# Long passes in the last feed-forward, a shift made on TensorE, and a new order of modulation units, in a two-block float32 model

## The chip, the cores and the metric

The kernel runs on one core of a Trainium2 chip. A core has five engines that each take their own instructions in order and meet through semaphores: TensorE (PE in the rows; its weight loads are PEld), VectorE (DVE), ScalarE (ACT), GpSimd (POOL) and SyncE (SP), and 16 DMA engines. The metric is the device time of one execution in microseconds (us); the kernel before takes 2502.35 us, the median of three runs (2498.07 to 2504.37).

## The reference

One sequence of 256 tokens of 1024 features, all in float32, passes two blocks. The first has two layers: a norm with a modulation, then attention (layer 0) or a gated DeltaNet (layer 1), and a feed-forward. The second block carries the 256 tokens and 256 context tokens through two layers of feed-forward, mixing (Fourier, convolution and latent attention) and feed-forward; the last layer leaves the context behind after its mixing.

```python
def first_block(...):
    cond = jax.nn.silu(c)
    for layer in range(DEPTH):
        mod = (cond @ ada_w[layer] + ada_b[layer])[:, None, :]
        shift_m, scale_m, gate_m, shift_f, scale_f, gate_f = jnp.split(mod, 6, axis=-1)
        h = rmsnorm(x, norm_mix_g[layer]) * (1.0 + scale_m) + shift_m
        ...
        x = x + gate_m * mixed
        h = rmsnorm(x, norm_ffn_g[layer]) * (1.0 + scale_f) + shift_f
        x = x + gate_f * swiglu(h, ffn_w_in[layer], ffn_w_out[layer])
    return rmsnorm(x, final_norm_g)

def ffn_half_step(s, m, i, norm_g, w_in, w_out):
    h = modulate(rmsnorm_2(s, norm_g), m, i)
    gu = h @ w_in
    y = (jax.nn.silu(gu[..., :D_FF]) * gu[..., D_FF:]) @ w_out
    return s + 0.5 * gate(m, i) * y
```

The feed-forward is 2816 wide. The modulations are products of one vector with a 1024 x 1024 matrix for each of 6 chunks a layer (first block) and of two vectors (tokens, context) for each of 9 (second block).

## The kernel before

**Tiles.** Activations lie with features on the 128 partitions: x is 8 tiles of 128 features by 256 tokens (512 columns where the context stands beside). A float32 product is made of three: each weight is split into a rounded part (hi, cast by ScalarE, L378) and the rest (lo, subtracted by VectorE, L379), each activation likewise, and `mm3` issues hi·hi (L405), hi·lo (L406) and lo·hi (L407) into one accumulator. So a group of one 128 x 128 weight tile and one activation tile takes three passes, of 256 columns for the tokens alone and 512 with the context.

**The stream of weights.** `plan()` writes one list of units of up to 128 x 1024 numbers (512 KB). SP's queue loads them in that order into a ring of 9 buffers (`pump`, L361, up to 12 units ahead), and the next three "mat" units are split. `get(key)` hands over the unit that a product needs; the list must be in the order of the calls. A "mod" unit is 128 columns of a modulation matrix: `mod_unit` (L480) has VectorE multiply it with the condition, spread over all partitions, and sum each row (L491, then a read of the accumulator); in the second block twice. `_evenly` (L48) puts the mod units between the mat units of a stage, `flush` works off those that stand next in the list before the next product is issued. Since VectorE takes its work in order, the place in the list decides what a mod product delays.

**Stages, by the profile's time.** Start, to 45 us: the condition is broadcast by one DMA to 128 partitions, the positions too; the first 16 units are the scale and the shift of layer 0's first norm; x is squared, POOL and VectorE add the squares; the first product reads h = x·scale·r + shift (`shift`, L855, with L860, L861). Attention to 180. First feed-forward to 380. Gated DeltaNet to 640: projections and heads 0 to 3 to 455, the inverse of their matrices together with heads 4 to 7 to 545, then z, the second inverse and the output. Feed-forward to 820. The second block's feed-forwards and mixings with 512 columns to 2290. The last feed-forward, for the tokens alone, to 2485, and the last norm.

**The last feed-forward** (`ffn`, L623, with `ns` = 1) multiplies the weights with x·gain, before it is divided by the root of the mean square; two more columns carry the shift (258 in all), and `act_raw` (L629) multiplies the result with r, adds the shift's column (copied by ScalarE, one column, L632) and applies the gate. The hidden width comes in thirds of 8, 7 and 7 tiles (j = 0 to 21); for each j a gate unit and an up unit, behind each third 8 output units (`project_out`, L602), whose result `resid` (L599) adds to x. The first two j are made together (`lead`). The last mixing's output projection (8 units of 8 tiles, on 256 columns) uses `project_out` as well. `push` (L532) squares each finished x tile on ScalarE and adds them on POOL; `rsq` (L515) makes r; `scaled` (L1404) multiplies each x tile with gain and r in one VectorE operation (L1409), and 8 DMAs write the result (L1522).

## Time and profile before

| | |
|---|---|
| runs, median (lowest to highest) | 2502.35 us (2498.07 to 2504.37) |
| profiled execution, its own time | 2497.55 us |
| span of the instructions in it | 2495.7 us |
| mean granted TensorE clock | 0.994 of 2.4 GHz |

All views below come from that one profiled execution; what lies around its span is 1.85 us. A row of a timeline is: start, duration, engine, line, operation, result and inputs by the program's names (numbers of buffers left out), and in brackets the time that the engine had waited and what released it. "x3" are instructions put together. A pass of TensorE is shown with its own length, from issue to end; passes overlap, so a stream's cost is the distance between starts. Busy time of an engine is not work that sets the end.

### The profile page before, as it was taken

To read this page: it belongs to the slowest core of one execution; us is meant where nothing else is said; L and a number is where in the kernel's file an instruction comes from. 1 tells how busy PE (TensorE), PEld (TensorE's weight loads), DVE (VectorE), ACT (ScalarE), POOL (GpSimd) and SP (SyncE) were. 2 spreads that over 40 slices of the span, in tenths; PEclk is the share of its full clock that TensorE was granted. 3 is DMA by queue.
4 is the path that set the end of the run, shared out by engine and by line. 5 is a ranking of instruction groups with operands and counts; after the bars stand their busy time and mean duration, and the time that the engine had idled before them with its cause. 6 is when DMAs were issued, how large, how long until landed. Compare 5 with 4: busy or idle time off the path is not lost.

```text
span 2495.7 us, 38415 instructions
## 1 busy us (share of the span) xinstructions
PE 2391.3 (96%) x14963; PEld 2130.3 (85%) x14963; DVE 1786.3 (72%) x3087; ACT 1073.5 (43%) x1879; POOL 169.9 (7%) x172
## 2 busy tenths in 40 slices
...
GB/s 332 271 223 227 225 236 225 153 102 90 263 265 209 161 236 191 173 162 99 79 79 33 85 219 178 153 182 87 109 201 180 160 175 95 83 131 77 205 183 70
DMA packets 118406, 412.21 MB, mean 165 GB/s; under 512 B 13136, under 2 KB 16464, under 8 KB 118224
## 3 DMA queue, kind: packets, MB, share of 16 engines
...
## 4 chain that ended last, share of the span: by engine, by line
PE 76%; DVE 9%; DMA 8%; issue 3%; ACT 2%; POOL 1%; DVEq 0%; ACTq 0%; SPq 0%; POOLq 0%
PE pmm L405 21%; PE pmm L406 21%; PE pmm L407 21%; DMA r<-w 7%; DVE l L379 2%; DVE r L491 2%; DVE junk L491 2%; PE pax L1026 2%; PE pmm L1348 1%; PE pax L407 1%; PE pax L406 1%; PE pax L405 1%; PE pnm L1387 1%; PE pax L1358 1%; ACT h L378 1%
## 5 line engine op out<-in xcount | busy, mean ns | idle before, releaser
L378 ACT CAST h<-r 128x1024 fp32r<-128x1024 f32 (+2 forms) x543 | 549.6, 1017 | 992.4 <-PE pmm L406 907.3
L379 DVE TENSOR_TENSOR l<-r,h 128x1024 fp32r<-128x1024 f32 (+2 forms) x543 | 645.0, 1192 | 195.6 <-ACT h L378 188.2
L405 PE MATMUL pmm<-h,h 128*128 128x512 f32 (+1 forms) x1916 | 668.3, 350 | 31.3 <-ACT h L860 23.1
L406 PE MATMUL pmm<-h,h 128*128 128x512 f32 (+1 forms) x1916 | 664.7, 347 | 1.8 <-DVE h L593 1.6
L407 PE MATMUL pmm<-h,l 128*128 128x512 f32 (+1 forms) x1916 | 662.3, 346 | 0.0
L405 PEld LDWEIGHTS pmm<-h,h 128*128 128x128 f32 x1916 | 364.1, 190 | 78.1 <-ACT h L860 23.8
L406 PEld LDWEIGHTS pmm<-h,h 128*128 128x128 f32 x1916 | 364.2, 190 | 48.5 <-DVE h L593 3.7
L407 PEld LDWEIGHTS pmm<-h,l 128*128 128x128 f32 x1916 | 364.2, 190 | 44.7 <-issue 0.2
L405 PE MATMUL pmm<-hid,h 128*128 128x256 f32 (+1 forms) x1053 | 349.8, 332 | 6.2 <-DVE s L633 2.7
L406 PE MATMUL pmm<-hid,h 128*128 128x256 f32 (+1 forms) x1053 | 348.3, 331 | 1.5 <-DVE hid L444 1.5
L407 PE MATMUL pmm<-hid,l 128*128 128x256 f32 (+1 forms) x1053 | 348.0, 331 | 0.7 <-DVE l L379 0.7
L405 PE MATMUL pmm<-hb,h 128*128 128x258 f32 x1008 | 286.4, 284 | 5.7 <-ACT hb L581 4.2
L407 PE MATMUL pmm<-hb,l 128*128 128x258 f32 x1008 | 284.9, 283 | 0.0
L406 PE MATMUL pmm<-hb,h 128*128 128x258 f32 x1008 | 284.9, 283 | 0.0
L491 DVE SCALAR_TENSOR_TENSOR junk<-r,cnd 128x1024 f32<-128x1024 f32 x144 | 175.9, 1221 | 125.9 <-DMA r<-w 122.6
L405 PEld LDWEIGHTS pmm<-hid,h 128*128 128x128 f32 x1053 | 200.4, 190 | 26.3 <-ACT hid L443 3.9
L406 PEld LDWEIGHTS pmm<-hid,h 128*128 128x128 f32 x1053 | 200.4, 190 | 20.9 <-DVE hid L444 2.4
L407 PEld LDWEIGHTS pmm<-hid,l 128*128 128x128 f32 x1053 | 200.5, 190 | 19.3 <-DVE l L379 1.1
L405 PEld LDWEIGHTS pmm<-hb,h 128*128 128x128 f32 x1008 | 190.8, 189 | 7.3 <-ACT hb L581 5.0
L406 PEld LDWEIGHTS pmm<-hb,h 128*128 128x128 f32 x1008 | 191.7, 190 | 0.4 <-DVE hb L582 0.2
L407 PEld LDWEIGHTS pmm<-hb,l 128*128 128x128 f32 x1008 | 191.7, 190 | 0.1
L491 DVE SCALAR_TENSOR_TENSOR r<-r,cnd 128x1024 f32<-128x1024 f32 x144 | 176.1, 1223 | 5.5 <-ACT cnd L464 2.4
...
## 6 DMA issues: line engine op xcount, KB each, us to landing
r<-w SPq DMA_DIRECT2D x665, 512.0 KB, 4.2
...
cnd<-cond ACTq DMA_DIRECT2D x8, 512.0 KB, 4.6
...
x<-xT ACTq DMA_DIRECT2D x8, 128.0 KB, 5.7
x<-ctxT ACTq DMA_DIRECT2D x8, 128.0 KB, 2.6
```

The lines of the kernel that those rows point to most:

```text
L378: nc.scalar.copy(h[:, :n], r[:, :n])
L379: nc.vector.tensor_tensor(lo[:, :n], r[:, :n], h[:, :n].bitcast(F32), op=OP.subtract)
L405: nc.tensor.matmul(out, wh, ah, start=start, stop=False)
L406: nc.tensor.matmul(out, wh, al, start=False, stop=False)
L407: nc.tensor.matmul(out, wl, ah, start=False, stop=stop)
L491: nc.vector.scalar_tensor_tensor(o, r, 1.0, self.conds[ns - 1 + s], op0=OP.mult, op1=OP.mult, accum_out=t[:, 8 * s + m:8 * s + m + 1])
L1026: nc.tensor.matmul(p[:, s], a[:, s], b[:, s], start=True, stop=True)
L1348: self.nc.tensor.matmul(s, q, k, start=True, stop=True)
L1358: self.nc.tensor.transpose(p[:, 128 * b:128 * b + 128], P[:, 128 * b:128 * b + 128], self.ident)
L1387: nc.tensor.matmul(o[64 * a:64 * a + 64, 128 * qt:128 * qt + 128], V[2 * s + b][:, h], pts[a][:, 128 * b:128 * b + 128], start=b == 0, sto ...
```

## The change

1. *Last feed-forward and last mix projection.* `wide` holds the two parts of an activation side by side as one tile of 512 columns. For each weight tile it issues one pass of hi with all 512 columns (L480: hi·hi in the left half, hi·lo in the right) and one of lo with 256 (L481, into the left half). The halves are added where the result is read: `act_wide` copies one half on ScalarE and adds on VectorE, `resid_wide` adds to x twice. It is used from j = 4 on; `enter_wide` makes the normalised activations for it. The last two output units of the last third and of the mix projection stay with three passes.
2. *Last norm.* x·gain is made on ScalarE for each tile as x is finished; behind r stand one product for each tile, six on VectorE and two (tiles 1 and 4) on POOL, and the output DMAs in another order.
3. *Start.* The condition and the positions are loaded as one row each and spread by a product with a row of ones. Each of the eight scale sums is finished as it comes. The eight shift units are loaded as rows of the matrix and multiplied on TensorE (`mod_rows`), four products of 32 rows by 256 columns each; a copy, two transposes and an addition bring the sum to its columns. The sums of squares are made on TensorE. The x tiles come over two queues. The first constants are loaded behind 19 units instead of first. The first projection's unit stands before the last two of the eight.
4. *Places of the mod units.* `_place` gives each stage's units a room, and spreads the mods by it. The chunk-2 mods of layer 1 (8 units) move from the DeltaNet into the first feed-forward. In the DeltaNet, heads 0 to 3 hold none instead of 10, heads 4 to 7 18 instead of 8, z 6 as before, the output none instead of 8. The second block's feed-forwards hold more of theirs among the output units.

The diff, cut to its core:

```diff
-def _evenly(units, mods, a, b):
-    n = len(units) - a - b
-    out, k = [], 0
-    for i, u in enumerate(units):
+def _place(units, mods, room):
+    room = [room(i, u[1]) for i, u in enumerate(units)]
+    out, k, c, total = [], 0, 0.0, sum(room)
+    for u, w in zip(units, room):
         out.append(u)
-        while k < len(mods) and i >= a + k * n // len(mods):
+        c += w
+        while k < len(mods) and c * len(mods) >= (k + 1 - 1e-6) * total:
             out.append(mods[k])
             k += 1
+    assert k == len(mods)
...
-    u += _evenly(q, A(0, 2, 3, 4), 4, 0)
+    rows = [("rows", ("ada_w", 0, 0, kt), [("ada_w", 0, kt * 128, 0, 1024)]) for kt in range(KT)]
+    u = A(0, 1) + rows[:6] + q[:1] + rows[6:] + _place(q[1:], A(0, 2, 3, 4), lambda i, key: float(i >= 3))
...
-    u += _evenly(q[:16], A(0, 5), 2, 3) + _evenly(q[16:], A(1, 0, 1), 0, MODS_OUT)
+    u += _place(q[:16], A(0, 5), _ffn_room(2, 15)) + _place(q[16:], A(1, 0, 1, 2), _ffn_room(0, 46))
...
-    u += _evenly(q, A(1, 2, 3, 4, 5), 0, 4)
...
+    u += _place(q, A(1, 3, 4, 5), lambda i, key: 2.0 if key[0] in "qkv" and key[1] > 3 else float(key[0] == "z"))
...
+    def wide(self, units, h):
+        ps = [(self.ax if i % 2 else self.mm)() for i in range(len(units))]
+        k = len(h)
+        for j, a in enumerate(h):
+            for u, p in zip(units, ps):
+                s = slice(128 * j, 128 * j + 128)
+                self.nc.tensor.matmul(p, u.hi[:, s], a.both, start=j == 0, stop=False)
+                self.nc.tensor.matmul(p[:, :T], u.lo[:, s], a[0], start=False, stop=j == k - 1)
+        return ps
...
-        if m == KT - 1:
+        if key[:3] == ("ada_w", 0, 1):
+            o, g = COLS["ada_b"][0] + KT + m, COLS["norm_mix_g"][0] + m
+            nc.vector.scalar_tensor_tensor(self.scale0[:, m:m + 1], t[:, m:m + 1], self.bias1[:, m:m + 1],
+                                           self.cols[:, g:g + 1], op0=OP.add, op1=OP.mult)
...
+    def mod_rows(self, key, r):
...
+            self.pmod = self.ax()
+        p = self.pmod
+        for g in range(4):
+            nc.tensor.matmul(p[32 * g:32 * g + 32, :256], self.cond0[:, kt, :], r[:, 256 * g:256 * g + 256],
+                             start=kt == 0, stop=kt == KT - 1)
+        if kt < KT - 1:
+            return
+        e, q = self.t("u"), self.ax()
+        nc.scalar.copy(e, p[:, :256])
+        for h in range(2):
+            nc.tensor.transpose(q[:, 128 * h:128 * h + 128], e[:, 128 * h:128 * h + 128], self.ident)
+        v = q[:, :256].rearrange("p (h g q) -> p g h q", h=2, g=4)
+        t = self.mod[key[:3]] = self.keep(KT, "mod_first")
+        o = COLS["ada_b"][0]
+        nc.vector.tensor_tensor(t.rearrange("p (g h) -> p g h", h=2), v[:, :, :, 0],
+                                self.cols[:, o:o + KT].rearrange("p (g h) -> p g h", h=2), op=OP.add)
     def gain(self, name, l, gname, ch):
         t = self.mod[name, l, ch]
...
+        if st["tensor"]:
+            n = st["n"][0] = st["n"].get(0, 0) + 1
+            if n == 1:
+                st["p"][0] = self.psum("nm", 1)[:, :T]
+            nc.tensor.matmul(st["p"][0], self.ones, s[:, :T], start=n == 1, stop=n == tot)
+            return
...
+        nc = self.nc
+        h = []
+        for k in range(KT):
+            t, a, b = self.t("t"), A[:, k:k + 1], B[:, k:k + 1]
+            nc.vector.scalar_tensor_tensor(t, self.x[k][:, :T], a, r, op0=OP.mult, op1=OP.mult)
+            p = Pair(self.t("hw", 512, F32R))
+            nc.scalar.activation(p[0], t, AF.Identity, bias=b)
+            nc.vector.scalar_tensor_tensor(p[1], t, b, p[0].bitcast(F32), op0=OP.add, op1=OP.subtract)
+            h.append(p)
+        return h
...
+    def resid_wide(self, m, p, gate):
+        v = self.x[m][:, :T]
+        for s in range(2):
+            self.nc.vector.scalar_tensor_tensor(v, p[:, s * T:s * T + T], gate[:, m:m + 1], v,
+                                                op0=OP.mult, op1=OP.add)
...
+        ps = self.wide([self.get(units(m)) for m in range(3)], src)
+        for m in range(KT):
+            if m < KT - narrow:
+                self.resid_wide(m, ps[m] if m < 3 else self.wide([self.get(units(m))], src)[0], gate())
+            else:
+                self.resid(m, self.gemm(self.get(units(m)), src, 0, T), 0, T, gate())
+            if st is not None:
+                self.push(st, self.x[m], 0, T)
     def project_out(self, units, src, ns, gate, st, tail=True):
...
+        def act_wide(j, pg, pu):
+            g, s = self.t("s"), self.t("s")
+            for p, v in ((pg, g), (pu, s)):
+                nc.scalar.copy(v, p[:, T:])
+                nc.vector.tensor_tensor(v, p[:, :T], v, op=OP.add)
+            self.act(g, g, AF.Silu)
+            nc.vector.tensor_tensor(s, s, g, op=OP.mult)
+            hid[j] = self.paired(s, "hid")
...
+            if wide:
+                hw = self.enter_wide(r, A, B)
...
+                if wide and j >= UNNORMED:
+                    act_wide(j, *(self.wide([self.get((key, x, j))], hw)[0] for x in "gu"))
+                    continue
...
-            self.project_out(lambda m: (key, "o", t, m), [hid[j] for j in range(j0, j1)], ns, gate,
-                             new if t == 2 else None, tail=t == 2)
+            units, src = lambda m: (key, "o", t, m), [hid[j] for j in range(j0, j1)]
+            if wide:
+                self.project_wide(units, src, gate, new if t == 2 else None, 2 if t == 2 else 0)
+            else:
+                self.project_out(units, src, ns, gate, new if t == 2 else None, tail=t == 2)
...
-        self.conds = [self.condition(0, right.tile([128, D], F32, name="cond")), None, None]
         self.phase("attn")
-        self.rope = self.rope_tables()
-        g0 = self.load_consts(0, "cst0")
-        self.c0 = g0
-        self.ident, self.ones, self.triu = g0["ident"], g0["ones"], g0["triu"]
...
+        rows = [self.t("og")[0:1, :] for _ in range(2)]
+        for i in range(2):
+            nc.scalar.dma_start(rows[i], a["cond"][0:1, 512 * i:512 * i + 512])
...
+        self.conds = [right.tile([128, D], F32, name="cond"), None, None]
+        for i in range(2):
+            p = self.mm()
+            self.spread_row(p, rows[i])
+            self.act(self.conds[0][:, 512 * i:512 * i + 512], p, AF.Silu)
...
-        st = self.stats()
+        st = self.stats(tensor=True)
...
+                r = self.rsq(st["p"][0], 1.0 / D)
+                self.rope = self.rope_tables()
                 self.flush(KT)
-                self.scale(st, self.gain("ada_w", 0, "norm_mix_g", 1))
+                self.c0 = self.load_consts(0, "cst0")
+                self.ident, self.triu = self.c0["ident"], self.c0["triu"]
+                self.scale(r, self.scale0)
                 self.flush()
+                self.ahead(("qa", 0))
...
-            st = self.ffn(("f2", l), st, 1 if last else 2, A, B, gate, None, conds=not last)
+            st = self.ffn(("f2", l), st, 1 if last else 2, A, B, gate, None, conds=not last, wide=last)
             self.dump(f"y{l}c")
-        for k, v in self.scaled(self.rsq(st["p"][0], 1.0 / D), "final_norm_2"):
-            (nc.sync if k % 2 else nc.scalar).dma_start(a["out"][:, k], v)
+        o = COLS["final_norm_2"][0]
+        for k, x in enumerate(self.x):
+            nc.scalar.activation(x[:, T:], x[:, :T], AF.Copy, scale=self.cols[:, o + k:o + k + 1])
+        r = self.rsq(st["p"][0], 1.0 / D)
+        for k, x in enumerate(self.x):
+            (nc.gpsimd if k in (1, 4) else nc.vector).tensor_tensor(x[:, T:], x[:, T:], r, op=OP.mult)
+        for k in (0, 2, 1, 3, 5, 4, 6, 7):
+            (nc.sync if k % 2 else nc.scalar).dma_start(a["out"][:, k], self.x[k][:, T:])
```

At the start, VectorE before: the last scaling of x by r and gain (x_153), splits of the first projection's weights (l), the last product of the shift (into mod_ada_w_0_243) and its bias, and then the first h.

```order
L853 SCALAR_TENSOR_TENSOR x_153<-x_153,gain_ada_w_1_222,r_224 128x256
L379 TENSOR_TENSOR l_203<-r_200,h_202 128x1024
L491 SCALAR_TENSOR_TENSOR r_197,mod_ada_w_0_243<-r_197,cond 128x1024
L379 TENSOR_TENSOR l_210<-r_207,h_209 128x1024
L379 TENSOR_TENSOR l_217<-r_214,h_216 128x1024
L499 TENSOR_TENSOR mod_ada_w_0_243<-mod_ada_w_0_243,cols 128x8
L379 TENSOR_TENSOR l_321<-r_241,h_320 128x1024
L861 SCALAR_TENSOR_TENSOR h_267<-x_139,mod_ada_w_0_243,h_267 128x256
```

VectorE after, at the same place: the scalings, splits, the addition that finishes the shift (mod_first), and then h.

```order
L1002 SCALAR_TENSOR_TENSOR x_112<-x_112,scale_145,r_174 128x256
L1002 SCALAR_TENSOR_TENSOR x_114<-x_114,scale_145,r_174 128x256
L400 TENSOR_TENSOR l_218<-r_215,h_217 128x1024
L400 TENSOR_TENSOR l_228<-r_225,h_227 128x1024
L594 TENSOR_TENSOR mod_first<-pax_320,cols 128x8
L400 TENSOR_TENSOR l_234<-r_231,h_233 128x1024
L1010 SCALAR_TENSOR_TENSOR h_326<-x_100,mod_first,h_326 128x256
L1010 SCALAR_TENSOR_TENSOR h_327<-x_102,mod_first,h_327 128x256
```

No product of the shift stands on VectorE any more. On TensorE they stand ahead of the first projection (pmm_350), the last two of eight units here, with the transposes (L590) behind them:

```order
L583 MATMUL pax_276<-r_221,og_86 32x256 x4
L583 MATMUL pax_276<-r_223,og_86 32x256 x4
L590 MATMUL pax_320<-const_254,u_319 128x128 x2
L443 MATMUL pmm_350<-h_326,h_217 128x256
L443 MATMUL pmm_377<-h_326,h_227 128x256
```

In the first inverse of the DeltaNet, VectorE before: the inverse's steps (dt), mod products (L491, inputs r and cond), a split.

```order
L1050 TENSOR_TENSOR dt_5180<-dt_5057,pax_5175 128x512
L491 SCALAR_TENSOR_TENSOR r_5337,mod_ada_w_4_5711<-r_5337,cond 128x1024
L1050 TENSOR_TENSOR dt_5187<-dt_5062,pax_5182 128x512
L491 SCALAR_TENSOR_TENSOR r_5462,mod_ada_w_4_5711<-r_5462,cond 128x1024
L491 SCALAR_TENSOR_TENSOR r_5520,mod_ada_w_4_5711<-r_5520,cond 128x1024
L491 SCALAR_TENSOR_TENSOR r_5646,mod_ada_w_4_5711<-r_5646,cond 128x1024
L1050 TENSOR_TENSOR dt_5307<-dt_5180,pax_5302 128x512
L1050 TENSOR_TENSOR dt_5314<-dt_5187,pax_5309 128x512
L379 TENSOR_TENSOR l_5583<-r_5330,h_5582 128x1024
```

The same steps of the inverse's levels (dt) after; qk are the convolutions of the next heads, L558 the mod products.

```order
L1199 TENSOR_TENSOR dt_5490<-dt_5361,pax_5485 128x512
L400 TENSOR_TENSOR l_5712<-r_5578,h_5711 128x1024
L1199 TENSOR_TENSOR dt_5497<-dt_5368,pax_5492 128x512
L558 SCALAR_TENSOR_TENSOR r_5392,mod_ada_w_4_5527<-r_5392,cond 128x1024
L558 SCALAR_TENSOR_TENSOR r_5452,mod_ada_w_4_5527<-r_5452,cond 128x1024
L558 SCALAR_TENSOR_TENSOR r_5515,mod_ada_w_4_5527<-r_5515,cond 128x1024
L558 SCALAR_TENSOR_TENSOR r_5523,mod_ada_w_4_5527<-r_5523,cond 128x1024
L1081 SCALAR_TENSOR_TENSOR qk_5513<-pmm_5587,cols,qk_5513 128x255
L1199 TENSOR_TENSOR dt_5622<-dt_5490,pax_5617 128x512
L1081 SCALAR_TENSOR_TENSOR qk_5513<-pmm_5587,cols,qk_5513 128x254
L1199 TENSOR_TENSOR dt_5629<-dt_5497,pax_5624 128x512
```

Each pair of steps is followed by a bunch of mod products as before, and there are convolutions of a head between the levels.

TensorE in the last feed-forward before, the last group of one unit (pmm_24027) and the first of the next: activations are hb, weights h and l.

```order
L405 MATMUL pmm_24027<-hb_21993,h_23951 128x258
L406 MATMUL pmm_24027<-hb_21993,h_23951 128x258
L407 MATMUL pmm_24027<-hb_21993,l_23952 128x258
L405 MATMUL pmm_24068<-hb_21993,h_23994 128x258
L406 MATMUL pmm_24068<-hb_21993,h_23994 128x258
L407 MATMUL pmm_24068<-hb_21993,l_23995 128x258
```

After, the same border of two units (hw holds both parts of an activation tile):

```order
L480 MATMUL pmm_23727<-hw_22221,h_23670 128x512
L481 MATMUL pmm_23727<-hw_22221,l_23671 128x256
L480 MATMUL pmm_23748<-hw_22186,h_23691 128x512
L481 MATMUL pmm_23748<-hw_22186,l_23692 128x256
L480 MATMUL pmm_23748<-hw_22191,h_23691 128x512
L481 MATMUL pmm_23748<-hw_22191,l_23692 128x256
```

Three passes a group have become two, a long and a short one.

## Rows read from the trace of the kernel before

**Rows 1.** Page, busy us (share of the span) and instructions of each engine
```profile
PE 2391.3 (96%) x14963; PEld 2130.3 (85%) x14963; DVE 1786.3 (72%) x3087; ACT 1073.5 (43%) x1879; POOL 169.9 (7%) x172
```

**Rows 2.** Windows: stretch, length, busy us of PE, PEld, DVE, ACT, POOL, clock, DMA share, GB/s
```profile
0.00:45.00 45.00, 2.43 (x5) 1.53 (x6) 33.41 (x70) 13.97 (x23) 4.97 (x9) 1.00 0.94 351
...
45.00:180.00 135.00, 129.48 (x936) 119.03 (x935) 122.19 (x223) 71.14 (x129) 12.64 (x13) 1.00 0.71 253
...
180.00:380.00 200.00, 193.99 (x1589) 192.38 (x1588) 153.95 (x246) 98.44 (x180) 7.24 (x6) 0.99 0.69 231
...
380.00:455.00 75.00, 58.74 (x426) 55.66 (x427) 69.93 (x141) 47.52 (x89) 0.97 (x1) 0.91 0.56 191
...
455.00:545.00 90.00, 88.12 (x699) 85.26 (x698) 71.30 (x134) 52.51 (x102) 33.92 (x31) 0.98 0.42 138
...
2290.00:2496.00 206.00, 195.28 (x1614) 193.56 (x1613) 131.57 (x205) 97.14 (x181) 4.93 (x5) 0.99 0.45 147
```

**Rows 3.** Lines of VectorE, 5 to 45 us: count, busy us, mean ns
```profile
L491 DVE SCALAR_TENSOR_TENSOR r<-r,cond 128x1024 f32<-128x1024 f32 x16 | 19.4, 1216 | 8.0 <-DMA r<-w 8.0
...
L491 DVE DVE_READ_ACCUMULATOR r<-r,cond 128x1 f32 x16 | 1.3, 80 | 0.0
```

**Rows 4.** Timeline, 33 to 45 us: start, us, engine, line, operation
```profile
33.12 1.04 ACT L378 CAST h<-r 128x1024 fp32r<-128x1024 f32 x1 [0.98 <-DMA r<-w]
...
36.96 1.04 ACT L378 CAST h<-r 128x1024 fp32r<-128x1024 f32 x1 [0.24 <-DMA r<-w]
...
40.47 1.21 DVE L491 SCALAR_TENSOR_TENSOR r<-r,cond 128x1024 f32<-128x1024 f32 x1
...
43.89 0.16 DVE L499 TENSOR_TENSOR mod_ada_w<-mod_ada_w,cols 128x8 f32<-128x8 f32 x1
...
44.64 1.01 PE L405 MATMUL pmm<-h,h 128*128 128x256 f32 x3 [23.09 <-ACT h L860]
```

**Rows 5.** DMA issues, 0 to 45 us: count, KB each, median us to landing
```profile
r<-w SPq DMA_DIRECT2D x28, 512.0 KB, 7.2
...
u<-pos ACTq DMA_DIRECT2D x1, 128.0 KB, 6.4
```

**Rows 6.** Timeline of TensorE, 1700 and 1400 us
```profile
1700.14 0.39 PE L405 MATMUL pmm<-h,h 128*128 128x512 f32 x1
...
1705.58 0.39 PE L405 MATMUL pmm<-h,h 128*128 128x512 f32 x1
...
1400.24 0.28 PE L405 MATMUL pmm<-h,h 128*128 128x256 f32 x1
...
1406.00 0.28 PE L405 MATMUL pmm<-h,h 128*128 128x256 f32 x1
```

**Rows 7.** Timeline, the tail
```profile
2473.26 1.34 POOL L551 TENSOR_TENSOR acc<-sq,sq 128x256 f32<-128x256 f32 x1 [183.57 <-ACT sq L536]
...
2481.16 0.74 POOL L551 TENSOR_TENSOR acc<-acc,sq 128x256 f32<-128x256 f32 x1 [1.78 <-ACT sq L536]
...
2484.86 0.59 PE L558 MATMUL pnm<-acc,const 128*128 128x256 f32 x2
...
2489.25 3.26 DVE L1409 SCALAR_TENSOR_TENSOR x<-x,cols,r 128x256 f32<-128x256 f32 x8
```

**Rows 8.** Timeline, entry of the gated DeltaNet
```profile
384.57 1.22 DVE L491 SCALAR_TENSOR_TENSOR r<-r,cond 128x1024 f32<-128x1024 f32 x1
...
387.49 1.22 DVE L491 SCALAR_TENSOR_TENSOR r<-r,cond 128x1024 f32<-128x1024 f32 x1
...
387.77 1.01 PE L405 MATMUL pmm<-h,h 128*128 128x256 f32 x3 [4.54 <-ACT h L592]
```

**Rows 9.** Waits over the span: us, times, longest us
```profile
DVE junk L491 <- DMA r<-w: 122.6, 73, 4.2
...
DVE r L491 <- DMA r<-w: 37.8, 23, 8.0
```

**Rows 10.** Lines of VectorE, 455 to 545 us
```profile
L491 DVE SCALAR_TENSOR_TENSOR r<-r,cond 128x1024 f32<-128x1024 f32 x13 | 16.6, 1285 | 6.5 <-DMA r<-w 6.5
```

134 lines of the change are left out of this document (93 added, 41 removed).

## The prediction

> **What bounds the kernel now.** I read the page's list of engines first [rows 1]: TensorE is busy in 96% of the span, VectorE in 72%, ScalarE in 43%. So time can come from three places only: TensorE's idle stretches, the number and form of its passes, and the two ends of the program. The table of windows says where TensorE waits [rows 2]. In the first 45 us it is busy 2.43 us, while VectorE has 33.41 us of work and the DMA engines are busy 94% of the time. In 380 to 455 us, the entry of the gated DeltaNet and its first four heads, it has 58.74 us of 75, with VectorE at 69.93. In the last 206 us it is busy for 195.28 us, and the rest lies in the tail; in the last feed-forward it never waits for long. So the start is bound by VectorE and the weight stream together, 380 to 455 by VectorE's chains, the last feed-forward by TensorE's passes.
>
> **The start.** Before, TensorE's first product begins at 44.64, released by ScalarE's h [rows 4]. Followed back: h waits for the shift's column sum (43.89), this for VectorE's last shift product (40.47), which stands in VectorE's order behind the eight scalings of x. The change takes the eight shift products off VectorE: 16 become 8, each 1.216 us and a read of 0.080 [rows 3], 8 x 1.296 = 10.4 us less. VectorE then has 33.4 - 10.4 = 23.0 us in this stretch and no longer ends last.
>
> What is late next is the weight stream. The casts in the timeline start 33.12, ..., 36.96 us, each released by its own DMA: three intervals of 1.28 us for one 512 KB unit [rows 4]. In the new order the last of the shift's eight "rows" units is the 17th unit, the place that the first projection's unit held before, which landed at about 33.1. Ahead of it, the 512 KB broadcast of the condition, the 128 KB broadcast of the positions and the 257 KB constants are gone or later: 0.9 MB, 0.9/0.512 x 1.28 = 2.2 us. It lands near 30.9. Behind it stand four fp32 products with 32 rows out, whose cost the trace doesn't show; the nearest row is an fp32 product with 128 rows, 0.59 us [rows 7], so between 0.6 (if they overlap) and 2.4 us; I take 2.4, since they stand in one queue. Then the copy, two transposes, an addition and the first h, about 0.4 us each by the 256-column rows of the tail, with a hand-over between them: some 2 us. 30.9 + 2.4 + 2 = 35.3, and 44.6 - 35.3 is **9.3, taken as 9.5 us** since the projection's splits are already done by then. Bounds: -12 if the stream starts earlier too, as the x tiles come over two queues; -4 if VectorE is held. That can happen: the cast of the position row stands in VectorE's order behind three scale products, and everything on VectorE behind it waits for a DMA that took 6.4 us from issue to landing [rows 5] and is now issued only after two squares. Does attention keep the gain? There VectorE works 122.19 us of 135 [rows 2], so 12.8 us of slack; the gain fits, barely.
>
> **The 512-column passes.** A stretch of 512-column rows has 24 intervals from 1700.14 to 1705.58, 0.2267 us each; 256-column rows have 48 from 1400.24 to 1406.00, 0.1200 each [rows 6]. Two halves cost 0.2400 in two passes and 0.2267 in one: a pass costs 13.3 ns beside its columns. Before, a group (one weight tile of 128 rows with one activation tile) has three short passes, 0.360 us; after it has one long and one short, 0.3467. Groups changed: 288 in gate and up, 64 + 56 + 42 in the three output thirds, 48 in the last mix projection, together 498. 498 x 13.3 ns = 6.6 us; since the last feed-forward's 258-column passes ran at 0.1195, a little faster, I take **-6.2**. A long and a short pass in turn never stand together in this trace: bounds 0 (no saving) and -6.6. A loss is excluded by the rows, as one weight load fewer goes with each group. The work added: 16 VectorE and 8 ScalarE operations that make the normalised activations beside the products of the first four column pairs, 28 more residual operations of 0.48 us, ScalarE copies of 256 columns for those of one. VectorE has 131.57 us of 206 and ScalarE 97.14 [rows 2], 74 and 109 us free; 21 and 13 us more are covered. If they weren't, the cost would show as waits of TensorE for hid.
>
> A rule speaks against this term. The Trainium skill (TensorE: Matmul & The Clock Gate, Back-to-back issue gap) gives a warm pass N/2.4 + 2.5 ns. By it a group saves 2.5 ns, and 498 of them 1.2 us instead of 6.2; the trace's 120.0 and 226.7 ns disagree with its 109 and 216, so I go by the trace.
>
> **The tail.** Before: after r, eight VectorE operations in 3.26 us, 0.41 each [rows 7], then the outputs. After: x times gain is made earlier on ScalarE, in gaps while TensorE finishes; behind r stand six products on VectorE and two on POOL. Two fewer are 2 x 0.41 = -0.8 if POOL runs at its 0.74 us with VectorE idle. But POOL's addition took 1.34 us while VectorE worked on two inputs. With two at 1.34 POOL ends at 2.7, near six of VectorE's 0.41, 2.5, and may slow it. **0, bounds -0.8 to +0.8.** The Trainium skill (SBUF — State Buffer, Terms) has the two engines exclude each other over the shared port pair. By it the sum is 6 x 0.41 + 2 x 0.74 = 3.9 us instead of 3.26, so +0.7; the 1.34 beside 0.74 agrees.
>
> **The modulation units moved.** A unit costs VectorE 1.285 + 0.08 in the DeltaNet [rows 3, 10]. Heads 0 to 3 lose ten. At the entry two such products stand within the chain to the first product (384.57, and 387.49 just after) while TensorE waits 4.54 us [rows 8]: without them about 2.4 us, and as TensorE's granted clock is 0.91 over this window, part of it at the lower of its levels, 1.2 GHz, **-3**. The output stage loses its eight: **-1**. Heads 4 to 7 get ten more: 13.7 us into VectorE's 90 - 71.3 = 18.7 idle, **+2** for those that stand before a step of the inverse. The first feed-forward gets eight: 10.4 us into 46 idle, **+0.7**. Sum **-1.3**; bounds -13 (all ten were on the path) and +10 (all 13.7 us in the inverse are, less the entry's gain). Later stages have so much VectorE time free that I give them nothing.
>
> **The sum.** -9.5 - 6.2 + 0 - 1.3 = -17.0 against the profiled execution's 2497.55, so 2480.5. That execution lies 4.8 us below the median of the runs, 2502.35, so the forecast is 2485.
>
> **The rivals.**
> A, as forecast: 2478 to 2490, chance 0.56.
> B, the start's gain is held by the position row or eaten in attention, whose VectorE is 91% busy: -4 instead of -9.5, 2491. For it: an order with a DMA in the middle; against: ring and slack. 0.17.
> C, 380 to 455 us is bound by VectorE throughout: the ten units' 13 us all come off the path, instead of 3: 2475. For it 69.93 of 75 busy; against it, in order work has idle parts that products fill. 0.18.
> D, the gap is no cost of a pass when long and short alternate, so the passes save 0 to 1: 2490. The rows of either kind speak against it. 0.04. The rule of the Trainium skill (TensorE: Matmul & The Clock Gate, Back-to-back issue gap) would make it 1.2, and nearly the same time.
> E, slower: VectorE takes its work in order, and a product whose unit has not landed holds everything behind it. The waits for weights are 122.6 + 37.8 us in 96 waits, 1.7 each [rows 9]. 18 units now stand in the inverse stretch: 18 x 1.7 = 30.6, less 6.5 waited there now [rows 10], and 13.7 of work make 37.8 us more against 18.7 - 6.5 = 12.2 idle: 26 us late instead of 2, 2509. The first feed-forward then holds 31 units: 31 x 1.7 of waits and 10.4 of work against 46 idle are 17 more at most, 2526; I put it at 2515. It decides once those idle 18.7 us are used up; against it, the DMA share there is 0.42. 0.05.
> A measurement of this kernel can tell some 0.3%, 7.5 us. Below 2494.8 lie C, most of A and B: 0.85. Within 0.3% are B's, A's and D's upper ends and a mild E: 0.11. Above 2509.9, E: 0.04. The range 2473 to 2496 goes from C to B and D together and leaves out E and the ends.
>
> **What would show it.** First full product at 35 to 36 us (wrong if past 40, then see VectorE's wait for the position row). Long passes 0.227 apart from the next short one, pairs 0.347; 0.36 means D. Idle before the DeltaNet's first product under 3 us, and 380 to 455 with 4 us fewer; 13 fewer means C. Waits of VectorE for weights in the inverse stretch: near 6.5 us right, over 20 is E. The whole is wrong if the span isn't 12 to 24 us shorter.

## The result: 29 us faster, 12 more than forecast

| | before | after |
|---|---|---|
| median (lowest to highest), runs | 2501.05 us (2498.07 to 2504.37), 4 | 2471.59 us (2470.25 to 2474.38), 4 |
| profiled execution, span | 2497.55, 2495.7 us | 2470.25, 2468.4 us |
| mean granted TensorE clock | 0.994 | 0.991 |

The ratio is 0.9883 [0.9866, 0.9900]. The forecast, 2485 with 2473 to 2496, had the direction and missed the size: the time lies 13 us under the forecast and below the range. Profiled against profiled, 27.3 us are gone, where the sum said 17.0.

The list of engines answers [rows 1]: 414 TensorE passes fewer are on record (the long passes take 498 away, the start adds some). VectorE works 2 us more in a span that is 27 us shorter.

```profile
PE 2397.8 (97%) x14549; PEld 2108.8 (85%) x14549; DVE 1788.5 (72%) x3119; ACT 1087.2 (44%) x1900; POOL 171.8 (7%) x171
```

The windows answer [rows 2]; the columns are the same.

```profile
0.00:45.00 45.00, 28.95 (x142) 16.02 (x143) 30.89 (x72) 22.14 (x37) 0.67 (x6) 0.77 0.96 366
45.00:180.00 135.00, 128.26 (x929) 117.17 (x928) 119.56 (x223) 73.06 (x135) 15.18 (x13) 0.99 0.70 247
...
380.00:455.00 75.00, 65.86 (x491) 63.48 (x490) 64.24 (x129) 44.27 (x84) 3.97 (x5) 0.93 0.44 141
455.00:545.00 90.00, 87.57 (x706) 84.71 (x705) 83.13 (x160) 58.80 (x119) 37.96 (x29) 1.00 0.51 167
```

In 380 to 455 TensorE works 65.86 us instead of 58.74. In 455 to 545, where the moved units went, VectorE is busy for 83.13 of 90 us instead of 71.30, and TensorE still for 87.57. That is the stage in which the rival "slower" was to show itself, so I read its mod products next, against [rows 10] (count, busy us, mean ns, idle before them):

```profile
L558 DVE SCALAR_TENSOR_TENSOR r<-r,cond 128x1024 f32<-128x1024 f32 x19 | 26.1, 1388 | 0.0
```

Nineteen products instead of 13, and none of them waited for its weights, where 6.5 us of waiting had stood before. The forecast took 6.5 us for right and over 20 for the rival; it is 0.

Windows hide where time is won when everything behind has moved. So I paired the TensorE instructions of the two traces that do the same work, and took the difference of their starts (after minus before, us):

```
at (before)   60   120   186   300   360   420   480   600   840  1240  1680  1980  2040  2220   end
difference  -8.8  -7.6  -9.9 -13.2 -10.0 -14.8 -11.0 -15.0 -15.0 -16.8 -14.9 -16.0 -20.9 -20.9 -27.3
```

Read as steps: the start -9; the way through the first feed-forward and the DeltaNet to 640 some -6, with swings of 3 to 4 us that are won and handed back; -5 at one single spot between 1980 and 2040; -6 in the last feed-forward. The first and the last were forecast. The two in the middle, 11 us, are what the forecast priced at 1.3.

How far one pair of traces can be trusted is seen from two of the runs below, `start_only` and `place_old`. They are the same program up to the last mixing, and still their traces lie 4.6 to 4.9 us apart from 640 to 1240. So a step of some 4 us in one pair says where to look, and the times decide what it is worth.

The spot, in the trace of before (timeline; a product of the condition, VectorE's product of the hidden tile, ScalarE's split of it, the output product that needs it):

```profile
1999.78 1.23 DVE L491 SCALAR_TENSOR_TENSOR junk<-r,cnd 128x1024 f32<-128x1024 f32 x1 [2.00 <-DMA r<-w]
...
2002.20 0.68 DVE L643 TENSOR_TENSOR s<-s,pmm 128x512 f32<-128x512 f32 x1
...
2002.91 0.62 ACT L443 CAST hid<-s 128x512 fp32r<-128x512 f32 x1 [4.94 <-DVE s L643]
...
2003.59 0.49 PE L405 MATMUL pmm<-hid,h 128*128 128x512 f32 x1 [2.29 <-ACT hid L443]
```

VectorE waits 2.00 us for a mod unit's weights, then works 2.4 us on it. Behind it stands the last activation of a third, and TensorE stands still for 2.29 us. The same place after. Counted through the list, the product at 1976.45 is that of the same unit, and it still stands ahead of the activation:

```profile
1976.45 1.23 DVE L558 SCALAR_TENSOR_TENSOR junk<-r,cnd 128x1024 f32<-128x1024 f32 x1 [0.79 <-DMA r<-w]
...
1981.30 0.69 DVE L784 TENSOR_TENSOR s<-s,pmm 128x512 f32<-128x512 f32 x1 [1.34 <-PE pmm L445]
...
1982.02 0.62 ACT L501 CAST hid<-s 128x512 fp32r<-128x512 f32 x1
```

So VectorE's order is what it was. What changed is when the weights land: before, the product begins 2.7 us behind the third's first output product on TensorE (1997.1); after, it begins 4.5 us ahead of it (1981.0), VectorE is through with it in time, and TensorE doesn't wait. In both lists the unit stands further back, in the next third: mod products run some ten places ahead of their place in the list.

### The profile page after: what moved, and what is told of

It is laid out like the page before. It is cut to its first block, busy times and chain, and to the rows that moved or that the text cites. A ratio compares the mean times of both kernels' runs of the same rounds, so it can differ in the third digit from the quotient of the medians.

```text
span 2468.4 us, 37696 instructions
## 1 busy us (share of the span) xinstructions
PE 2397.8 (97%) x14549; PEld 2108.8 (85%) x14549; DVE 1788.5 (72%) x3119; ACT 1087.2 (44%) x1900; POOL 171.8 (7%) x171
## 4 chain that ended last, share of the span: by engine, by line
PE 84%; DVE 7%; DMA 5%; ACT 2%; issue 2%; POOL 1%; DVEq 0%; ACTq 0%; SPq 0%; POOLq 0%
PE pmm L444 21%; PE pmm L443 21%; PE pmm L445 21%; DMA r<-w 5%; PE pmm L480 4%; PE pmm L481 2%; DVE l L400 2%; PE pax L1175 1%; DVE r L558 1%; PE pmm L1500 1%; PE pax L444 1%; PE pax L445 1%; PE pax L443 1%; PE pnm L1539 1%; PE pax L1510 1%
## 5 line engine op out<-in xcount | busy, mean ns | idle before, releaser
L443 PE MATMUL pmm<-h,h 128*128 128x512 f32 (+1 forms) x1876 | 656.9, 351 | 7.3 <-ACT h L692 3.5
L444 PE MATMUL pmm<-h,h 128*128 128x512 f32 (+1 forms) x1876 | 652.5, 349 | 1.4 <-DVE h L693 1.2
L443 PEld LDWEIGHTS pmm<-h,h 128*128 128x128 f32 x1876 | 356.6, 191 | 53.5 <-ACT h L692 3.9
L444 PEld LDWEIGHTS pmm<-h,h 128*128 128x128 f32 x1876 | 356.7, 190 | 47.0 <-DVE h L693 3.0
L443 PE MATMUL pmm<-hid,h 128*128 128x512 f32 (+1 forms) x913 | 309.8, 339 | 5.2 <-DVE s L765 1.7
L444 PE MATMUL pmm<-hid,h 128*128 128x512 f32 (+1 forms) x913 | 308.3, 338 | 0.7 <-DVE hid L502 0.7
L445 PE MATMUL pmm<-hid,l 128*128 128x512 f32 (+1 forms) x913 | 308.3, 338 | 0.4 <-DVE l L400 0.4
L558 DVE SCALAR_TENSOR_TENSOR junk<-r,cnd 128x1024 f32<-128x1024 f32 x144 | 176.2, 1223 | 132.8 <-DMA r<-w 129.7
L443 PE MATMUL pmm<-hb,h 128*128 128x258 f32 x720 | 204.6, 284 | 4.3 <-ACT hb L681 3.0
L444 PE MATMUL pmm<-hb,h 128*128 128x258 f32 x720 | 203.8, 283 | 0.0
L445 PE MATMUL pmm<-hb,l 128*128 128x258 f32 x720 | 203.6, 283 | 0.0
L443 PEld LDWEIGHTS pmm<-hid,h 128*128 128x128 f32 x913 | 173.3, 190 | 24.7 <-ACT hid L501 1.9
L444 PEld LDWEIGHTS pmm<-hid,h 128*128 128x128 f32 x913 | 173.3, 190 | 20.1 <-DVE hid L502 1.7
L445 PEld LDWEIGHTS pmm<-hid,l 128*128 128x128 f32 x913 | 173.3, 190 | 18.7 <-DVE l L400 0.6
L558 DVE SCALAR_TENSOR_TENSOR r<-r,cnd 128x1024 f32<-128x1024 f32 x144 | 176.3, 1224 | 5.2 <-ACT cnd L527 2.3
L712 DVE SCALAR_TENSOR_TENSOR x<-pmm,mod_w_mod,x 128x256 f32<-128x256 f32 x164 | 73.0, 480 | 126.1 <-PE pmm L445 126.0
L443 PEld LDWEIGHTS pmm<-hb,h 128*128 128x128 f32 x720 | 136.3, 189 | 5.5 <-ACT hb L681 3.7
L444 PEld LDWEIGHTS pmm<-hb,h 128*128 128x128 f32 x720 | 136.9, 190 | 0.5 <-DVE hb L682 0.4
```

Of the source, the lines that this page charges most:

```text
L443: nc.tensor.matmul(out, wh, ah, start=start, stop=False)
L444: nc.tensor.matmul(out, wh, al, start=False, stop=False)
L445: nc.tensor.matmul(out, wl, ah, start=False, stop=stop)
L558: nc.vector.scalar_tensor_tensor(o, r, 1.0, self.conds[ns - 1 + s], op0=OP.mult, op1=OP.mult, accum_out=t[:, 8 * s + m:8 * s + m + 1])
L712: self.nc.vector.scalar_tensor_tensor(v, p[:, s * T - c0:s * T + T - c0], gate[:, 8 * s + m:8 * s + m + 1], v, op0=OP.mult, op1=OP.add)
```

## The experiments

Two theories stood against each other. P: the extra time is the mod units' places. Q: places are worth the forecast's 1 to 3 us, and the start or the long passes brought more than forecast. Every kernel was timed in rounds with the kernel before; the number behind a time is its ratio to that one, with its interval in brackets. Differences to the changed kernel are between medians, and those of one kernel move by some 2 us from one set of rounds to the next.

### Which part brought it

The changed kernel with all mod units at their old places (the lines of `plan()` again with `_evenly`):

```diff
-    u += _place(q, A(1, 3, 4, 5), lambda i, key: ...)
+    u += _evenly(q, A(1, 2, 3, 4, 5), 0, 4)
```

> The changed kernel with the modulation units of every stage at their old places (start, long passes and last norm stay as changed). Theory P (the 12 us beyond the forecast come from the places of the modulation units: in the aligned traces TensorE gains about 5 us at the entry of the DeltaNet, 5 us at the end of a third in the feed-forward near 2000 us, 2 us elsewhere): the time rises by 11 to 13 us against the changed kernel, to about 16 us under the kernel before. Theory Q (the earlier start keeps the weight stream ahead, so that later waits for weights go away; the places are worth the 1.3 us forecast): it rises by 0 to 3 us, 26 to 29 us under the kernel before.

2483.74 us, ratio 0.9938 [0.9922, 0.9955]: 12 us given up. Q fell. The other way round, the kernel before with nothing but the new places:

```diff
-    u += _evenly(q, A(1, 2, 3, 4, 5), 0, 4)
+    u += _place(q, A(1, 3, 4, 5), lambda i, key: ...)
```

> The kernel before with the modulation units at their new places and nothing else changed. P: 11 to 13 us faster than the kernel before. Q: 0 to 3 us faster.

2489.82, 0.9959 [0.9945, 0.9973]: by the ratio 10 us won by places alone, by the medians of the same rounds 9. The kernel before with the changed start alone (the changed kernel with `_evenly` everywhere, three passes and the old last norm):

> The changed start alone: old places of the modulation units, three passes in the last feed-forward, the old last norm. P: 9 to 10 us faster than the kernel before, the gain at the first product carried unchanged to the end. Q: 20 to 23 us faster.

2491.39, 0.9964 [0.9951, 0.9978]: 9 us won by the ratio, 7.5 by the medians. And the changed kernel with three passes in the last feed-forward and mix:

```diff
-            st = self.ffn(("f2", l), st, 1 if last else 2, A, B, gate, None, conds=not last, wide=last)
+            st = self.ffn(("f2", l), st, 1 if last else 2, A, B, gate, None, conds=not last, wide=False)
```

> The changed kernel with three passes in the last feed-forward and mix projection. If long passes save 12 to 13 ns a group, it is 6 us slower than the changed kernel, 23 us under the kernel before; if a long and a short pass in turn save only a few ns, it is as fast as the changed kernel within 1.5 us.

2477.69, 0.9910 [0.9895, 0.9925]: 6.1 us given up. Last, the old last norm in the changed kernel:

```diff
+        for k, v in self.scaled(self.rsq(st["p"][0], 1.0 / D), "final_norm_2"):
+            (nc.sync if k % 2 else nc.scalar).dma_start(a["out"][:, k], v)
```

> The changed kernel with the old last norm (eight products on VectorE behind r, outputs in the old order). As forecast, 0 within 0.8 us of the changed kernel. If POOL's two products come beside VectorE's without loss, it is 0.8 us slower; if the two engines hold each other up, 0.7 us faster.

2469.71, 0.9876 [0.9860, 0.9893], no difference that can be measured. So the start brought 7.5 to 9, the places 9 to 12, the passes 6 and the norm 0, together 23 to 27 of the 29.

### Which places

Old places in the first feed-forward and the DeltaNet only:

```diff
-    u += _place(q[:16], A(0, 5), _ffn_room(2, 15)) + _place(q[16:], A(1, 0, 1, 2), _ffn_room(0, 46))
+    u += _evenly(q[:16], A(0, 5), 2, 3) + _evenly(q[16:], A(1, 0, 1), 0, MODS_OUT)
...
-    u += _place(q, A(1, 3, 4, 5), lambda i, key: ...)
+    u += _evenly(q, A(1, 2, 3, 4, 5), 0, 4)
```

> The changed kernel with the modulation units of the first feed-forward and of the DeltaNet alone at their old places. Theory P (most of what the places give comes from these two stages; with all old places the aligned trace had lost 11.9 us by 640 us): 8 to 12 us slower than the changed kernel. Rival R (the later feed-forwards carry it, near 2000 us above all): 0 to 4 us slower.

2478.59, 0.9911 [0.9896, 0.9925]: 7.0 given up, below P's 8 to 12 and above the rival's 0 to 4. Most of the places' gain comes from these two stages, and not all of it. Old places in the second block's first feed-forward of its second layer only (the stage of the spot; the expectations give it as 1410 to 2130 us, but in the changed kernel's trace it runs from 1761 to 2127):

```diff
-    u += _place(_ffn_units(("f1", 1), ...), B(1, 4, 5, 6, 7, 8), _ffn_room(6, 60))
+    u += _evenly(_ffn_units(("f1", 1), ...), B(1, 4, 5, 6, 7, 8), MODS_IN, MODS_OUT)
```

> The changed kernel with the old places in the feed-forward from 1410 to 2130 us alone. In the first pair of traces TensorE lost 4.9 us at one spot near 2005 us in the kernel before (a modulation product that waits for its weights stands ahead of the last activation of a third; the granted clock then falls); with all old places on the changed kernel only 1.1 us there. If the wait costs every time and the clock falls only in some executions: 1 to 3 us slower. If the spot costs what the first pair shows: 5 us slower.

2474.82, 0.9899 [0.9884, 0.9913]: 3.2 given up by the medians, which is not clear of noise, as the interval overlaps that of the changed kernel. In the trace 4.7 are lost at the spot, where the rows are those of before again:

```profile
1983.46 1.23 DVE L571 SCALAR_TENSOR_TENSOR junk<-r,cnd 128x1024 f32<-128x1024 f32 x1 [2.00 <-DMA r<-w]
...
1985.88 0.68 DVE L797 TENSOR_TENSOR s<-s,pmm 128x512 f32<-128x512 f32 x1
...
1986.59 0.62 ACT L514 CAST hid<-s 128x512 fp32r<-128x512 f32 x1 [4.72 <-DVE s L797]
...
1987.26 0.50 PE L456 MATMUL pmm<-hid,h 128*128 128x512 f32 x1 [2.07 <-ACT hid L514]
```

The stall is 2.07 us and 0.45 for the next pass. The rest of the 4.7 is in the clock, which the windows show (the last four numbers: POOL, clock, DMA share, GB/s):

```profile
1970.00:1987.00 17.00, 15.19 (x68) 12.23 (x66) 12.81 (x23) 4.36 (x6) 0.00 (x0) 1.00 0.46 155
1987.00:1991.00 4.00, 3.28 (x9) 2.34 (x10) 2.80 (x5) 1.15 (x2) 0.00 (x0) 0.71 0.78 260
1991.00:2000.00 9.00, 9.00 (x39) 7.43 (x38) 6.78 (x12) 0.95 (x1) 0.00 (x0) 0.94 0.43 142
```

Behind the stall the granted clock falls from full to 0.71 and then 0.94, a part of either stretch at 1.2 GHz. In passes at full clock that is an estimated 0.29 x 4 + 0.06 x 9 = 1.7 us lost; with 2.07 and 0.45 it makes 4.2 of the 4.7.

The loss isn't the same each time. Four traces have the old order here, and TensorE's wait for this activation is 2.29 us in the kernel before, 2.07 in `f11_old`, 0.62 in `start_only` and 0.08 in `place_old`, where the clock stays full. Paired with traces of the new order, the spot costs 4.9, 4.7, 1.6 and 1.1 us. With the new order (`after`, `place_only`, `f0gdn_old`) TensorE doesn't wait there. The expectation had left room for this.

### Is it the unit ahead of the last activation?

Theory M: one mod unit in the wrong place makes the stall, and moving it one place in the list brings it back. Theory O: it takes a queue of units so dense that the weights come late, and one of them ahead of the activation. First the changed kernel with one unit moved from behind the first output unit to directly behind the last up unit of that third:

```diff
+    u[i], u[i + 1] = u[i + 1], u[i]
```

> The changed kernel with one modulation unit moved by one place: in the second third of the feed-forward from 1410 to 2130 us, from behind the first output unit to behind the last up unit, so that its two products stand on VectorE ahead of the last activation of the third. Theory M (it is this one place: the product waits for its weights, the last hidden tile is late, TensorE waits and its granted clock falls): 3 to 5 us slower than the changed kernel, all of it near 1990 us. Theory N (the load of modulation units in that third as a whole does it): 0 to 1 us slower.

2472.64, 0.9900 [0.9885, 0.9915], and no stall at the spot. That doesn't test M: counted through the list, the moved unit's product ran at 1920.21, 60 us ahead of the spot (in the changed kernel at 1921.32). The place in the list isn't the place on the engine, and the unit at the spot was left alone. Then the opposite, no mod unit behind any third's last up unit:

> The changed kernel with no modulation unit directly behind the last up unit of any third: in seven thirds the unit moves by one place, behind the first output unit, or in two of them ahead of the last up unit. M: at these thirds TensorE's starts are late by 1.5, 0.9, 2.1, 0.5, 2.5, 2.1 and 2.0 us in the changed kernel's trace, together 11.6: 8 to 12 us faster than the changed kernel, about 2461. N: within 2 us of it.

2475.07, 0.9908 [0.9893, 0.9924]: nothing won either, and in the trace 4 us lost in the first feed-forward. The units behind the last up units run earlier than the thirds' ends too, so this run doesn't test M any better; it only shows that moving these seven units wins nothing. Third, `f11_old` with just the two units around that up unit moved behind the first output unit:

```diff
+    u.insert(o + 1, u.pop(i + 3))
+    u.insert(i + 3, u.pop(i + 1))
```

> The changed kernel with the old places in the feed-forward from 1410 to 2130 us, as in the run that cost 4 us, but with the two modulation units behind the last gate and the last up unit of its second third moved behind the third's first output unit. Theory O (the unit behind the last gate unit lands late, its product is VectorE's next instruction ahead of the last activation): the stall of 3 us and the low clock after it near 1985 us go, 0 to 1 us slower than the changed kernel. Theory N (so many units in that third make the weight stream late at its end, whichever stands last): the stall stays, 3 to 5 us slower.

2474.52, 0.9906 [0.9888, 0.9924]. The row of the spot is now

```profile
1982.75 0.50 PE L461 MATMUL pmm<-hid,h 128*128 128x512 f32 x1 [0.60 <-ACT hid L519]
```

0.60 us instead of 2.07, no low clock, and 1.6 us late at that point against the changed kernel instead of 4.7. That is what O expects, but it doesn't show O: the two moved units ran at 1918.29 and 1928.41, the unit at the spot kept its place and still waited 1.91 us for its weights, ahead of the activation, and `start_only` has 0.62 us there with nothing moved. The edit and chance can't be told apart. The time, between 2468.74 and 2475.49 in four runs, doesn't tell the 3 us apart either. So M, as one place in the list, is untested, and what stands is the row's reading: TensorE is late when the unit that VectorE has reached lands late.

The other half of O, that late weights matter at all, was tried by taking one buffer from the ring. SP's loads wait for VectorE to be through with an earlier unit in it; its longest waits after the change (us, times, longest):

```profile
SPq L387 <- DVE l L400: 1295.1, 425, 27.5
SPq L387 <- DVE r L558: 425.6, 180, 17.4
```

The edit:

```diff
-    RAW, SPL = 9, 5
+    RAW, SPL = 8, 5
```

> The changed kernel with a ring of 8 weight buffers instead of 9. If late landing of units is what makes the modulation products wait (a load is issued when VectorE has finished with the unit nine places ahead), the waits of VectorE's products for weights grow from some 110 us and TensorE stalls at the ends of thirds: 5 to 15 us slower. If the stream has slack and only the order on VectorE counts: within 2 us.

2485.20, 0.9951 [0.9935, 0.9967]: 13.6 us lost. VectorE's waits for units with 8 buffers (us in total, times, longest):

```profile
DVE junk L558 <- DMA r<-w: 137.8, 82, 4.3
DVE r L558 <- DMA r<-w: 28.5, 22, 3.5
```

In the changed kernel:

```profile
DVE junk L558 <- DMA r<-w: 129.7, 74, 4.8
DVE r L558 <- DMA r<-w: 20.7, 21, 3.6
```

And in `place_old`:

```profile
DVE junk L570 <- DMA r<-w: 119.6, 76, 3.8
DVE r L570 <- DMA r<-w: 33.1, 26, 3.1
```

The first two differ by 16 us, near the 13.6 lost. But the last two, 150.4 and 152.7 in all, differ by 2, with 12 us between their times: the sum of the waits doesn't set the time, so it must matter which product waits. The trace with 8 buffers has a plain case, with the list of the changed kernel unaltered. There one product starts at 908.85 without a wait, and TensorE doesn't wait for the activation behind it. With 8 buffers the product of the same unit waits 3.25 us:

```profile
921.04 1.23 DVE L558 SCALAR_TENSOR_TENSOR junk<-r,cnd 128x1024 f32<-128x1024 f32 x1 [3.25 <-DMA r<-w]
...
922.19 0.68 DVE L784 TENSOR_TENSOR s<-s,pmm 128x512 f32<-128x512 f32 x1
...
923.58 0.50 PE L443 MATMUL pmm<-hid,h 128*128 128x512 f32 x1 [1.13 <-ACT hid L501]
```

TensorE waits 1.13 us and 0.59 for the next pass, some passes behind it are 0.63 us long instead of 0.39, and the trace loses 3.9 us here. This is the mechanism of the spot, made by the edit to the ring alone. Where the rest of the 13.6 is lost wasn't followed.

### Which places in the DeltaNet

Units put back step by step into the stage that the change had emptied. Ten between the entry and heads 3, as before, eight in heads 4 to 7, none in the output:

```diff
+    u += _place(q, A(1, 3, 4, 5), lambda i, key: 10 / 13 if i < 13 else 8 / 12 if i < 25 else 0.75 * (key[0] == "z"))
```

> The changed kernel with ten modulation units again in the DeltaNet's entry and heads 0 to 3, eight in heads 4 to 7 and six beside z; the output holds none and the first feed-forward keeps its 32. Theory P1 (the products within the norm's chain at the entry carry the gain: 4 to 5 us between the first feed-forward's last product and 410 us, clock included): 4 to 7 us slower than the changed kernel. P2 (the inverse and the freed output stage carry it): 0 to 2 us slower, or faster, as the inverse gets relief.

2479.54, 0.9918 [0.9904, 0.9932]: 7.9 lost. Against the changed kernel the trace is 2.4 us late at 360, 9.9 at 418, 7.1 at 445, 10.8 at 518, and 10.7 at the end of the stage (paired by the count of products of the same kind, since TensorE's order differs here): lost at the entry, 3 us of it handed back in heads 0 to 3, and lost again by 518. So I asked whether it is the three units listed at the entry (behind ab, q0, k0) or the seven behind them:

```diff
+    g0 = [k for k, x in enumerate(u) if x[1] == ("ab",)][0]   # heads_seven: ("v", 0), and [:7]
+    ms = [k for k, x in enumerate(u) if k > g0 and x[0] == "mod"][:3]
+    taken = [u[k] for k in ms]
+    u = [x for k, x in enumerate(u) if k not in ms]
+    for i, x in enumerate(taken):
+        u.insert(g0 + 1 + 2 * i, x)
```

Three:

> The changed kernel with three modulation units moved from heads 4 to 7 to the DeltaNet's entry, behind its first three units as before the change. Theory P1 (these three products stand in the norm's chain and in the making of h): 4 to 7 us slower between the first feed-forward's end and 410 us, with 7 to 10 us of low clock there instead of 3.3; less some 1 us of relief in the inverse. Rival (heads 0 to 3, not the entry, carry what the ten units cost): 0 to 2 us slower.

Seven:

> The changed kernel with seven modulation units moved from heads 4 to 7 into heads 0 to 3, none at the entry. P1: 2 to 4 us slower by 445 us, less 1 to 2 us given back in the inverse: 0 to 3 us slower. Rival: 5 to 8 us slower.

2471.14, 0.9891 [0.9875, 0.9907], and 2471.65, 0.9894 [0.9879, 0.9909]: neither loses anything. The run with three doesn't test P1, though: the three ran at 343.91, 349.26 and 353.81, ahead of the entry, as products run ahead of their place in the list, and the first product waited 3.53 us as in the changed kernel. With seven, three mod products (from 371.58 on) did stand ahead of the first product in the norm's chain, and it came 3.4 us later than after (378.90 against 375.52):

```profile
374.75 1.22 DVE L564 SCALAR_TENSOR_TENSOR r<-r,cond 128x1024 f32<-128x1024 f32 x1
...
376.22 1.22 DVE L564 SCALAR_TENSOR_TENSOR r<-r,cond 128x1024 f32<-128x1024 f32 x1
...
378.90 1.01 PE L449 MATMUL pmm<-h,h 128*128 128x256 f32 x3 [5.49 <-ACT h L698]
```

By 450 us, still in heads 0 to 3, that was given back. Ten from v0 on (the same edit with `[:10]`):

> The changed kernel with ten modulation units moved from heads 4 to 7 into heads 0 to 3, behind v of head 0 and each unit after it; none directly at the DeltaNet's entry. With three units at the entry, or seven in heads 0 to 3, the time stayed that of the changed kernel (2471 to 2472 us), with ten in both it rose by 8. Theory S (the stretch from the entry to the inverse takes about seven products on VectorE, more come on the path, wherever they stand): 5 to 9 us slower than the changed kernel. Theory T (ten cost only with three of them at the entry): 0 to 2 us slower.

2472.94, 0.9901 [0.9885, 0.9918]: 1.3, within what can be told. The trace is 2.1 us late at the first product, 7.2 at 418, 3.0 at 445, 3.8 at the end of the stage and 2.2 at the end of the program. Then the other end of the stage, ten units in heads 4 to 7 and eight in the output, as before:

```diff
+    u += _place(q, A(1, 3, 4, 5), lambda i, key: 10 / 12 if 13 <= i < 25 else 0.75 if 25 <= i < 33 else 8 / 12 if 33 <= i < 45 else 0.0)
```

> The changed kernel with ten modulation units in heads 4 to 7, six beside z and eight in the DeltaNet's output, instead of 18, 6 and none. If products in the output stage delay it, 1 to 3 us slower than the changed kernel; if they are hidden there and the inverse gets relief, 0 to 2 us faster.

2477.19, 0.9915 [0.9901, 0.9930]: 5.6 lost. By the count of products the trace is 1.3 us late by 520, 1.9 by 545, 3.1 by 557, and 5.8 by 563, between the first two products of the second inverse. VectorE's mod products there:

```profile
518.12 1.23 DVE L558 SCALAR_TENSOR_TENSOR r<-r,cond 128x1024 f32<-128x1024 f32 x1 [2.61 <-DMA r<-w]
...
525.39 1.22 DVE L558 SCALAR_TENSOR_TENSOR r<-r,cond 128x1024 f32<-128x1024 f32 x1 [0.63 <-DMA r<-w]
...
554.44 1.74 DVE L558 SCALAR_TENSOR_TENSOR r<-r,cond 128x1024 f32<-128x1024 f32 x1
...
558.22 1.71 DVE L558 SCALAR_TENSOR_TENSOR r<-r,cond 128x1024 f32<-128x1024 f32 x1
```

The first two stand in the chain of z's norm and wait for weights, the others in the second inverse, where a product takes 1.7 us and TensorE waits 2.61 us for its first step instead of 1.13. Most of the loss is in the second inverse. Before, the products stood there in the same way. After, VectorE's last mod product of the stage starts at 514.79: the second inverse has none.

The pair before and after, counted in the same way, agrees. TensorE is 10.0 us earlier at 376, 14.0 at 404 and 9.4 at 454, so the stretch from 380 to 455, emptied of ten products, gave nothing that stayed. It is 11.3 earlier at 523, 13.4 at 534, 13.3 at 570 and 15.0 at 579: z's norm and the second inverse, from where the output's units had gone, kept theirs.

### Can it be bettered?

The start's constants, for which the transposes wait 2.09 us, issued ahead of the scale sums (`load_consts` before `self.flush(KT)`); and this with `off_u` and the old last norm together:

> The changed kernel with the first constants' DMA issued ahead of the shift's units that stood before it. In the changed kernel's trace the two transposes of the shift wait 2.1 us at 33.9 us for these constants. If nothing else is late there, TensorE's first full product comes 1.5 to 2 us earlier and the time is 1 to 2 us lower; if the weight stream, now 0.5 us later, or VectorE's splits are next, it gains 0 to 0.5.

Together:

> The two edits before together, and the last norm as it was in the kernel before. M: about 10 to 14 us faster than the changed kernel (2458 to 2462). N: 1 to 3 us faster.

2471.24, 0.9895 [0.9878, 0.9911], and 2471.73, 0.9898 [0.9883, 0.9912]. TensorE is 1.5 us earlier at 43 us with the first, and attention has eaten it by 120. No version tried beats the changed kernel by more than the measurement can tell.

The changed kernel has a stall of the same kind left, in the second feed-forward of the second block's first layer:

```profile
1616.49 1.23 DVE L558 SCALAR_TENSOR_TENSOR junk<-r,cnd 128x1024 f32<-128x1024 f32 x1 [4.60 <-DMA r<-w]
...
1619.03 0.50 PE L443 MATMUL pmm<-hid,h 128*128 128x512 f32 x1 [1.47 <-ACT hid L501]
```

In `heads_ten` TensorE has no such wait there, though its list is the same from that stage on. No version tried moves this unit.

## Why the prediction missed

**The start, -9.5: right.** First full product forecast at 35.3, found at 35.39 (against 44.64 in [rows 4]):

```profile
30.76 1.08 PE L583 MATMUL pax<-r,og 128*32 128x256 f32 x8 [0.20 <-DMA r<-w]
33.93 0.66 PE L590 MATMUL pax<-const,u 128*128 128x128 f32 x2 [2.09 <-DMA const<-const]
35.39 1.01 PE L443 MATMUL pmm<-h,h 128*128 128x256 f32 x3 [0.80 <-ACT h L1009]
```

The weight stream set it, as the forecast said. That the sum came out to 0.1 us is partly luck: the 2.09 us for the constants weren't in it, and the last unit's four products (each leaves two of the eight records) took 1.1 us together, where 2.4 were taken. By the times the start brought 7.5 to 9. Rival B (a hold by the position row) didn't come; attention gave back 2 us and had them again at its output.

**The long passes, -6.2: right.** A long and a short pass in turn:

```profile
2313.18 0.39 PE L480 MATMUL pmm<-hw,h 128*128 128x512 f32 x1
2313.41 0.28 PE L481 MATMUL pmm<-hw,l 128*128 128x256 f32 x1
...
2318.04 0.39 PE L480 MATMUL pmm<-hw,h 128*128 128x512 f32 x1
```

Fourteen pairs from 2313.18 to 2318.04, 0.347 each, as forecast from [rows 6]. `wide_off` gave 6.1 us. The rule of the Trainium skill (TensorE: Matmul & The Clock Gate, Back-to-back issue gap), which the page gives for a pass by itself, would make a pair an estimated 325 ns, and the saving 1.2; the trace disagrees with both.

**The tail, 0: right.** Six products beside POOL's two take as long as eight alone [rows 7]:

```profile
2461.97 3.16 DVE L1696 TENSOR_TENSOR x<-x,r 128x256 f32<-128x256 f32 x6
2462.01 1.83 POOL L1696 TENSOR_TENSOR x<-x,r 128x256 f32<-128x256 f32 x2 [6.87 <-DVE r L618]
```

0.53 us each instead of 0.41. The rule of full exclusion (Trainium skill, SBUF — State Buffer, Terms) had given 3.9 us in all; the trace lies between that and no effect, 2.5.

**The modulation units' places, -1.3: this step failed.** They brought 9 to 12 us. Three sentences of it were wrong.
- "Later stages have so much VectorE time free that I give them nothing." Measured 3.2 us by the medians (`f11_old`, not clear of noise), and 1.1 to 4.9 at the spot in the traces. VectorE's idle time there doesn't help: one unit whose weights land some 2 us late, ahead of one activation that ends a third, costs a stall and at times the clock behind it. The rows were in the trace of before, at 2000; I had looked at shares by stage and not for TensorE's single waits behind VectorE.
- "The output stage loses its eight: -1", and "+2 for those that stand before a step of the inverse". With the eight back there and ten instead of 18 in heads 4 to 7, 5.6 us are lost (`out_eight`), most of it in the second inverse. The ten products more in heads 4 to 7 and the inverse cost no 2 us: in the pair before and after, TensorE is some 2 us earlier at 523 than at 454.
- "At the entry ... -3", from two products in the chain to the first product. The wait shrank less than forecast (4.54 us became 3.53, where under 3 was to be the sign), TensorE was 4.8 us earlier at 410, and 3.8 of that were handed back by 480. Seven or ten products put back behind v0 cost 0 to 1.3 us, since most of it is given back by 450; the arrangement with three listed at the entry and seven behind them cost 7.9.

The bounds of the term, -13 to +10, did hold it. 2473, where the range began, is about what the sum gives with the places at -13 and all else as forecast; the start's own bound was not added. Rival E counted 31 units in the first feed-forward, where there are 32, which changes nothing.

Rival C gave 2475, the nearest number, with the reason that the ten units' 13 us are all on the path from 380 to 455. So its nearness is luck, and the reason fell: TensorE, 10.0 us ahead at 376, was 9.4 ahead at 454, and ten units put back in heads 0 to 3 cost 1.3 us (`heads_ten`). The rival "slower" fell with the 0.0 of waiting in the inverse.

**Open.** Why three units listed at the entry and seven behind them cost 8 us, when three, seven or ten alone cost at most 1.3; the stages give back differently, and no run separates that. How much of the gain in later stages is the spot, as the times don't tell 3 us apart. Where the 2 us between 840 and 1240 come from: there the passes of before are 2 ns longer each, with nothing in the trace that explains it.
